# Layer 0 of a two-layer decoder step: the small products between the dense ones moved to three places of every eight, and two kinds of transposes given full shape

## The chip, the core and the metric

The kernel runs on one core of a Trainium2 chip. The metric is the time of one execution on the device in microseconds (us). The core has five engines that work side by side: TensorE (PE, the matrix products), VectorE (DVE), ScalarE (ACT), GpSimd (POOL) and SyncE (SP, which issues most DMA transfers). Each works through its own list of instructions in order; semaphores make one engine wait for another.

## What is computed

One inference step of a decoder with two layers, over 1024 prompt tokens behind 16 meta tokens, and 8 sample sequences of 8 tokens, so 1104 tokens with a model width of 1024. Layer 0, which the change touches, is a gated DeltaNet: one input projection gives q, k (8 heads of 128), v and z (16 heads of 128); q, k and v go through a causal convolution over 4 tokens; then a delta rule runs in chunks, and its outcome is normed, gated with z and projected.

```python
def gdn_mixer(xn, S0, conv_buf, w_in, conv_w, a_log, dt_bias, gn_w, w_out, segments):
    proj = xn @ w_in
    ...
    qkv, new_buf = causal_conv(qkv, conv_buf, conv_w)   # conv_buf: the 3 rows before, of each sequence
    q = l2norm(q) * 128 ** -0.5 ; k = l2norm(k)         # heads repeated: 2 value heads share one key head
    beta = sigmoid(b) ; g = -exp(a_log) * softplus(a + dt_bias)
    o, S = gdn_chunked(q, k, v, g, beta, S, chunk)
    o = rmsnorm(o, gn_w) * silu(z)
    return o @ w_out, S, new_buf

# gdn_chunked, per chunk:
L = strict(kb @ k.T * decay) ; A = L + I                # A is inverted by blocks
v_new = u - w @ S
o = q_dec @ S + attn @ v_new
S = S * exp(g_last) + k_dec.T @ v_new                   # the recurrence from chunk to chunk
```

Layer 1 is an RWKV-7 layer, which the change leaves as it is.

## The kernel before

Layer 0 works through eight pairs of value heads (j = 0 to 7), each pair with its one key head. Tokens lie in three segments of 384, 384 and 336. A pair has six column tiles of the input projection: q of this pair, two tiles of v, two of z, and k of the next pair. A tile of 128 columns and one segment is a **dense product**: eight chunks of the width, three matmuls each (the fp32 numbers are split into a high and a low part, and the product low by low is left out), 24 matmuls with 384 or 336 moving columns. They fill PE nearly without end, and everything else that PE has to do is put between them.

This is done with numbered **gaps**. `dense_gaps` calls `L.gap()` behind each six dense matmuls, and the class `Gaps` then runs what was put at that number, in the order of the priorities given. A pair has 6 x 3 x 4 = 72 gaps; pair j begins at gap B = 24 + 72j. Everything of the small work is a list of such numbers, written by hand:

- the **recurrence** of pair j (`recur_plan`) starts at R0 = B + 60 and takes 8 gaps for each of its nine steps of 128 tokens (6 gaps for j = 7). In a step PE has three places: `rA<-S,K`; three gaps on `rA<-X,TT` and `rA<-S,Q`; two gaps on `rA<-w,ktok`, `rA<-w,attn` and `mktok` (the transpose of K). B is a multiple of eight, so the three are the gap numbers with a remainder of 4, 7 and 1 by eight. DVE makes X (L1039) from the first, the state S (L1072) and o (L1093) from the others, and the next step's `rA<-S,K` reads S.
- `conv_plan` transposes the three history rows of the 8 sample sequences, 24 rows of 128 (`fhist`), and the last rows of each tile, 27 wide (`flast`), and DVE and ACT run the convolution (`cvy`, L634) and SiLU (L641).
- `prep_plan` makes the products of K with itself (`usc`, "squares"), from which DVE takes norms (L752) and E (L766), which go through an inverse by blocks; 18 blocks of 31 and 32 rows are worked on POOL (j > 0) or DVE (j = 0 and the most of 7), and the **merges** (`uU`, `fU`, `uY`, `fY`) put them together with products of 32x32 and 64x64.
- `values_done` transposes v (`f<-vt`); `query_norms` transposes q (`fss`); `sample_read_plan` reads the states of the sample sequences against their keys and queries (`usr`, 128x32 stationary, in four gaps with eight calls each, two passes per call); `sample_write_plan` writes them (`msw`, `fsw`); `msc` are the scores q by k; `gdn_norm_out` transposes o for the norm (`mog`), and DVE gates it (`zg`, L1142).

A product that PE issues goes to one of five kinds of PSUM buffers: "d" (two, dense), "f" (two), "u" (one), "m" (one), "r" (two). The letter at the front of a name in the profile is the kind: `usc` and `usr` both need the single "u". fp32 products issue two passes per call, transposes one.

At the program's start the first rows are normed, and POOL sets T1n (a zeroed buffer for the merges, L708) and kqm (L711) to zero in `gdn_zero`.

Of the kernel before, what the change touches and what calls it, by code (L numbers as in the profile page):

```python
# [25 lines left out]
class Gaps:  # L26
# [62 lines left out]
class Builder:  # L89
# [496 lines left out]
    def conv_plan(self, ends, ft, dst, done=None):  # L586
# [12 lines left out]
        def load():  # L599
            c.hist = t(fp, [24, 128], "hist", 2)  # L600
            nc.sync.dma_start(c.hist, i["state_gdn_conv"][0].rearrange("b r c -> (b r) c")[:, f])

        def head():
            x = t(fp, [128, 411], "raw", 3)
            raws.append(x)
            hp = self.ps("f", 2, "hist")
            self.transpose(hp[:, 0:24], c.hist)
            nc.vector.tensor_copy(v11(x)[:, :, 0:3], v3(hp[:, 0:24]))
            nc.gpsimd.memset(x[:, 88:91], 0.0)
# [13 lines left out]
        def first(s):  # L623
            ys.append(t(fp, [128, 408], "cvy", 2))
            self.act(ys[s][:, 0:wd(s)], raws[s][:, 0:wd(s)], AF.Identity, scale=cw[0])
            if s == 0:
                c.last = t(fp, [128, 27], "last", 2)
                nc.gpsimd.tensor_copy(v3(c.last[:, 0:24]), v11(raws[0])[:, :, 8:11])
            elif s == 2:
                nc.gpsimd.tensor_copy(c.last[:, 24:27], prev(2))  # L630
# [19 lines left out]
        def ending():  # L650
            lp = self.ps("f", 2, "last")
            self.transpose(lp[0:27, 0:128], c.last)
            c.ls = t(fp, [27, 128], "lasts", 1)
            nc.vector.tensor_copy(c.ls, lp[0:27, 0:128])
# [4 lines left out]

        L.put(ends[0] - 11, load, 2)  # L660
        L.put(ends[0] - 2, head, 2)
        for s, e in enumerate(ends):
            L.put(e + 1, lambda s=s: first(s), 1.5)
            L.put(e + 2, lambda s=s: tap(s, 1, 2), 2)
            L.put(e + 3, lambda s=s: tap(s, 3), 2)
            L.put(e + 4, lambda s=s: tanh(s), 2)
            L.put(e + 5, lambda s=s: silu(s), 1.7)
            if done is not None:
                L.put(e + 8, lambda s=s: done(s), 2.2)
        L.put(ends[2] + 5, ending, 2.5)  # L670
        L.put(ends[2] + 8, store, 3)
        return out
# [33 lines left out]
    def gdn_zero(self):  # L706
        self.T1n = self.t(self.fp, [128, 18, 64], "T1n")
        self.nc.gpsimd.memset(self.T1n, 0.0)  # L708
# [23 lines left out]
    def prep_plan(self, j, B, G, o, pace):  # L732
# [11 lines left out]
        def squares(s):  # L744
            if s == 0:
                c.kq, c.rec, c.bp = t(fp, [128, 9], "kq", 2), t(fp, [128, 9], "rec", 2), t(fp, [128, 9, 2], "bp", 2)
            p = p_[s] = self.ps("u", 1, "sc")
            for tt in range(3):
                b = slice(128 * tt, 128 * tt + 128)
                self.mm(p[:, b], G.K[s][:, b], G.K[s][:, b])  # L750
            for tt in range(3):
                nc.vector.scalar_tensor_tensor(p[:, 384:512], p[:, 128 * tt:128 * tt + 128], 1.0, self.ident, op0=ALU.mult, op1=ALU.mult,  # L752
                                               accum_out=c.kq[:, 3 * s + tt:3 * s + tt + 1])
# [22 lines left out]
        for s in range(3):  # L776
# [58 lines left out]
        v = lambda p, k: p[:, 0:6 * k].rearrange("p (c i) -> p c i", i=k)  # L835
        half = lambda s: (("u", 1), ("f", 2), ("u", 1))[s]

        def merge(s):
# [31 lines left out]
            self.act(TT[0:64, :, 64:128], v(p, 64)[0:64], AF.Identity, scale=-1.0)  # L870
        for s, at in enumerate((0, 1, 4)):
            m = merge(s)
            for u in range(4):
                L.put(i0 + 8 + at + u, lambda m=m: next(m, None), 1)
                L.put(i0 + 8 + at + u, lambda m=m: next(m, None), 1.05)

    def values_done(self, G, h, s):
        nc = self.nc
        p = self.ps("f", 2)
        for tt in range(3):  # L880
            self.transpose(p[:, 128 * tt:128 * tt + 128], G.V[:, 128 * tt:128 * tt + 128])
        if h == 0:
# [25 lines left out]
    def sample_read_plan(self, j, B, G):  # L908
# [22 lines left out]
        def out():  # L931
            S = G.sS = t(self.gp, [64, 2, 256], "sS", 1)
            for x in (0, 1):
                nc.scalar.copy(S[:, x], c.ps[64 * x:64 * x + 64, 0:256])
        for g, x in ((12, (0, 0)), (14, (0, 1)), (15, (1, 0)), (22, (1, 1))):
            L.put(B + g, lambda x=x: load(*x), 3)
        L.put(B + 14, spread, 2.6)
        for g, x in ((18, (0, (0, 1))), (19, (0, (2, 3))), (26, (1, (0, 1))), (27, (1, (2, 3)))):
            L.put(B + g, lambda x=x: mults(*x), 2.5)
        L.put(B + 28, out, 2.5)  # L940

    def sample_write_plan(self, j, G, h, r):
# [27 lines left out]
        def store(g):  # L970
            nc.sync.dma_start(self.o["s_gdn"][0, 4 * g:4 * g + 4, hv].rearrange("b k v -> k b v"), Sb[g])
        at = (1, 4 if h else 2, 1, 4, 5, 7, 8, 10, 12) if j < 7 else (1, 2, 1, 3, 4, 5, 5, 7, 9)
        for u, f in zip(at, (lambda: load(0), lambda: load(1), lambda: spread(0, 1, 2, 3), lambda: scale(0, 0, 1), lambda: scale(0, 2, 3),
# [3 lines left out]
    def recur_plan(self, j, R0, G, sp):  # L977
# [1152 lines left out]
    def layer0(self, top, right, xa, xc):  # L2130
# [75 lines left out]
        with tc.manual_schedule(engines=self.every):  # L2206
# [14 lines left out]
            for j, g in enumerate(G):  # L2221
# [462 lines left out]
```

## Time and profile before

| | |
|---|---|
| runs | 2162.58, 2164.77, 2170.14 us, median 2164.77 |
| profiled execution | 2173.22 us, its span 2171.5 us, mean granted clock of PE 0.984 |
| PE busy | 2072.0 us, 95% of the span |
| DVE, ACT, POOL busy | 1483.7 (68%), 1247.0 (57%), 1199.7 us (55%) |
| layer 0's dense products | from about 20 to 1153 us of the span |
| chain that ended last | PE 62%, DVE 17%, DMA 7%, ACT 7% |

The profiled execution is 0.39% over the median. In rows of a timeline, the first number is the start in us, the second the time from the start of the first to the end of the last of the group; a bracket at the end gives how long the engine sat idle before it and what released it. Matmuls overlap, so that the price of a group is read from the starts of its neighbours. L126 is a transpose on PE, L129 a product. `128*32` is the stationary operand, `128x384` the moving one.

### The profile page before, as it was taken

What the parts mean: (1) busy time and instruction counts of PE and PEld (TensorE: products, weight loads), DVE (VectorE), ACT (ScalarE), POOL (GpSimd) and SP (SyncE); (2) the same over time, 40 slices, a digit from 0 to 9 for tenths busy, and PEclk for the clock granted to TensorE, in tenths of its full rate; (3) what the DMA queues carried; (4) which work ended last, traced back from release to release, by engine and by line L of the source; (5) the groups of instructions that cost most, each with busy time, mean ns of one, the idle gap of its engine ahead of it and who ended that gap; (6) DMA issues with size and microseconds to landing.
All of it is one profiled execution on the core that took longest, in us unless ns stands there. A gap on an engine that the chain in (4) does not pass through costs nothing.

```text
span 2171.5 us, 56154 instructions
## 1 busy us (share of the span) xinstructions
PE 2072.0 (95%) x20958; PEld 1935.4 (89%) x20958; DVE 1483.7 (68%) x3761; ACT 1247.0 (57%) x3622; POOL 1199.7 (55%) x1784
## 2 busy tenths in 40 slices
PE   8889999999999999988999999999998989999997
PEld 7879989899898989887999999999888988899886
DVE  7878586675758576795534682578865637899976
ACT  6536565665656565655533374665654437777763
POOL 3418768585858678523432362217866335777751
PEclk9999999999999999999999999999999999999998
DMA  4324242424334242425435225478786576767642
GB/s 123 82 65 129 69 117 79 112 77 119 99 87 121 75 120 75 111 74 163 149 100 150 76 64 175 160 236 249 203 241 180 154 190 180 208 179 194 170 132 88
DMA packets 510764, 291.68 MB, mean 134 GB/s; under 512 B 240777, under 2 KB 495866, under 8 KB 510490
## 3 DMA queue, kind: packets, MB, share of 16 engines
q1 hardware_dynamic: 510490, 288.08, 47.1%
q8 instruction: 166, 2.72, 0.5%
q14 instruction: 108, 0.88, 0.1%
HBM read 195.66 MB, written 92.30 MB: 133 GB/s over the span
## 4 chain that ended last, share of the span: by engine, by line
PE 62%; DVE 17%; DMA 7%; ACT 7%; issue 3%; POOL 2%; SPq 2%; DVEq 0%; POOLq 0%; ACTq 0%
PE d L129 13%; PE dv L129 8%; PE dz L129 7%; PE rA L129 6%; PE do L129 3%; DVE cvy L634 2%; PE rA L133 2%; PE dk L129 2%; PE dq L129 2%; PE zo L129 2%; DMA wraw<-in_gdn_w_out 1%; PE xX L133 1%; DVE invtmp L690 1%; DVE invT L692 1%; PE dlora L129 1%
## 5 line engine op out<-in xcount | busy, mean ns | idle before, releaser
L143 POOL TENSOR_TENSOR wlo<-wraw,whi 128x512 fp32r<-128x512 f32 x174 | 231.9, 1333 | 211.8 <-ACT whi L139 181.0
L634 DVE SCALAR_TENSOR_TENSOR cvy<-raw,cw,cvy 128x408 f32<-128x408 f32 (+2 forms) x288 | 201.0, 698 | 31.5 <-ACT cvy L115 27.6
L692 POOL TENSOR_TENSOR invT<-invT,invtmp 72x31 f32<-72x31 f32 (+27 forms) x310 | 196.3, 633 | 24.3
L690 POOL TENSOR_TENSOR invtmp<-invA,invT 72x31 f32<-72x31 f32 (+27 forms) x310 | 186.9, 603 | 21.7 <-DMA invA<-rltd 3.7
L129 PE MATMUL d<-xc,whi 128*128 128x384 f32 (+1 forms) x640 | 175.8, 340 | 0.5 <-ACT ev L1441 0.5
L139 ACT CAST whi<-wraw 128x512 fp32r<-128x512 f32 x238 | 146.2, 616 | 37.3 <-DMA wraw<-in_rwkv_w_rkvz 14.5
L129 PE MATMUL dv<-xc,whi 128*128 128x384 f32 (+1 forms) x480 | 154.5, 343 | 0.0
L129 PE MATMUL dz<-xc,whi 128*128 128x384 f32 (+1 forms) x480 | 152.0, 339 | 0.0
L115 ACT ACTIVATE w<-rA,nbp 128x128 f32<-128x128 f32 x144 | 45.2, 364 | 152.5 <-PE rA L129 140.0
L129 PEld LDWEIGHTS d<-xc,whi 128*128 128x128 f32 x640 | 117.2, 190 | 2.6 <-ACT ev L1441 0.9
L129 PE MATMUL d<-xc,wlo 128*128 128x384 f32 (+1 forms) x320 | 104.5, 337 | 1.3 <-DVE wlo L143 1.3
L160 POOL TENSOR_TENSOR ors<-ovar,cvals 128x6 f32<-128x6 f32 x24 | 34.1, 1421 | 125.1 <-DVE ovar L1122 125.1
L129 PE MATMUL dv<-xa,whi 128*128 128x384 f32 (+1 forms) x288 | 102.7, 357 | 0.0
L129 PE MATMUL dz<-xa,whi 128*128 128x384 f32 (+1 forms) x288 | 102.1, 354 | 0.5 <-DVE zg L906 0.5
L129 PE MATMUL d<-xa,whi 128*128 128x384 f32 (+1 forms) x336 | 95.4, 337 | 1.1 <-POOL xa L143 1.0
L1953 POOL TENSOR_SCALAR y<-y,mv,grs 128x64 f32<-128x64 f32 x132 | 83.8, 653 | 17.6 <-DVE grs L164 16.0
L959 POOL TENSOR_SCALAR Sb<-Sb,eglb 128x128 f32<-128x128 f32 x128 | 89.5, 711 | 6.4 <-DMA Sb<-in_state_gdn 4.1
L129 PEld LDWEIGHTS dv<-xc,whi 128*128 128x128 f32 x480 | 89.3, 189 | 3.5 <-issue 3.0
L129 PEld LDWEIGHTS dz<-xc,whi 128*128 128x128 f32 x480 | 89.5, 189 | 0.6 <-issue 0.2
L143 DVE TENSOR_TENSOR wlo<-wraw,whi 128x512 fp32r<-128x512 f32 x64 | 49.4, 772 | 50.3 <-ACT whi L139 38.7
L129 PE MATMUL d<-xh,whi 128*128 128x384 f32 (+1 forms) x256 | 82.3, 333 | 0.8 <-ACT xh L139 0.8
L129 PE MATMUL d<-xl,whi 128*128 128x384 f32 (+1 forms) x256 | 82.6, 335 | 0.3 <-DVE sal L1584 0.3
(558 smaller groups left out, 7345.6 us busy)
## 6 DMA issues: line engine op xcount, KB each, us to landing
wraw<-in_gdn_w_in SPq DMA_DIRECT2D x96, 256.0 KB
wraw<-in_rwkv_w_rkvz SPq DMA_DIRECT2D x74, 256.0 KB
Sb<-in_state_gdn SPq DMA_DIRECT2D x64, 256.0 KB
wraw<-in_rwkv_w_o SPq DMA_DIRECT2D x48, 256.0 KB
E<-drow SPq DMA_DIRECT2D x24, 384.0 KB
attn<-drow SPq DMA_DIRECT2D x24, 384.0 KB
wraw<-in_gdn_w_out SPq DMA_DIRECT2D x36, 256.0 KB
out_s_gdn<-Sb SPq DMA_DIRECT2D x32, 256.0 KB
```

The costliest lines, as they stand in the source:

```text
L115: return self.nc.scalar.activation(out, in_, func, bias=bias, scale=scale, **kw)
L129: self.nc.tensor.matmul(out, lhsT, rhs, start=start, stop=stop)
L133: self.nc.tensor.matmul(out, lhsT, rhs, start=start, stop=True, skip_group_check=True)
L139: nc.scalar.copy(hi, x)
L143: e.tensor_tensor(lo, x, hi.bitcast(F32), op=ALU.subtract)
L160: self.nc.gpsimd.tensor_tensor(y, x, half.broadcast_to(sh), op=ALU.pow)
L634: nc.vector.scalar_tensor_tensor(ys[s][:, 0:wd(s)], raws[s][:, k:k + wd(s)], cw[k], ys[s][:, 0:wd(s)], op0=ALU.mult, op1=ALU.add)
L690: v.tensor_tensor(tmp, A[:, j, j + 1:32].unsqueeze(2).broadcast_to([nb, n, m]), Tv[:, j, 0:m].unsqueeze(1).broadcast_to([nb, n, m]), op=AL ...
L692: v.tensor_tensor(Tv[:, j + 1:32, 0:m], Tv[:, j + 1:32, 0:m], tmp, op=ALU.subtract)
L959: nc.gpsimd.tensor_scalar(Sb[g][:, u], Sb[g][:, u], self.eglb[:, hv, 4 * g + u:4 * g + u + 1], None, op0=ALU.mult)
L1953: nc.gpsimd.tensor_scalar(y[:, q], y[:, q], mv[:, q, 0:1], P.rs[:, q:q + 1], op0=ALU.subtract, op1=ALU.mult)
```

## The change

- A helper `on(g)` moves a gap number up to the next with a remainder of 1, 4 or 7 by eight. The transposes of v, the last rows and the query norms are put there.
- The history rows and the last rows get four persistent tiles of 128x128, zeroed by POOL in `gdn_zero`, used in turn. The history product becomes a full product with the tile as stationary operand and 24 columns of the identity moving (two passes instead of one of 24 rows), and `flast` a transpose to 128 rows.
- The squares of segments 0, 1, 2 go from B - 2, B + 2, B + 6 to B - 1, B + 4, B + 7 (j > 0), those of segment 2 into the kind "f".
- The merges of pairs 1 to 6 go from B + 56 to B + 63 (four gaps in a row for each segment, overlapping) to gaps from B + 57 to B + 71, those of segment 2 into "f"; pair 0's go there as well.
- The sample reads take two gaps with 16 calls instead of four with 8; their loads come one gap later.
- The sample writes, the scores and the norm's transposes are shifted by a gap or two, with other priorities, and v has a buffer for each segment.

```diff
+def on(g):
+    while g % 8 not in (1, 4, 7):
+        g += 1
+    return g
...
-            c.hist = t(fp, [24, 128], "hist", 2)
-            nc.sync.dma_start(c.hist, ...)
+            c.hist = self.hists[0]
+            self.hists.reverse()
+            nc.sync.dma_start(c.hist[0:24], ...)
...
-            self.transpose(hp[:, 0:24], c.hist)
+            self.mm(hp[:, 0:24], c.hist, self.ident[:, 0:24])
...
-            self.transpose(lp[0:27, 0:128], c.last)
+            self.transpose(lp[:, 0:128], c.last)
...
-        L.put(ends[0] - 11, load, 2)
-        L.put(ends[0] - 2, head, 2)
+        L.put(max(ends[0] - 11, 3), load, 2)
+        L.put(ends[0] - (3 if ends[0] % 24 == 15 and ft < 16 else 2), head, 2)
...
-                L.put(e + 8, lambda s=s: done(s), 2.2)
-        L.put(ends[2] + 5, ending, 2.5)
-        L.put(ends[2] + 8, store, 3)
+                L.put(on(e + 8), lambda s=s: done(s), 2.2)
+        L.put(on(ends[2] + 5), ending, 2.5)
+        L.put(on(ends[2] + 5) + 3, store, 3)
...
         self.nc.gpsimd.memset(self.T1n, 0.0)
+        self.hists = [self.t(self.fp, [128, 128], f"hist{x}") for x in (0, 1)]
+        self.lasts = [self.t(self.fp, [128, 128], f"last{x}") for x in (0, 1)]
+        for x in self.hists + self.lasts:
+            self.nc.gpsimd.memset(x, 0.0)
...
-            p = p_[s] = self.ps("u", 1, "sc")
+            p = p_[s] = self.ps(*(("f", 2) if j and s == 2 else ("u", 1)), "sc")
...
-            k = B - 2 + 4 * s + o
+            k = B + (-1, 4, 7)[s] if j else B - 2 + 4 * s + o
...
-        for s, at in enumerate((0, 1, 4)):
+        for s in range(3):
             m = merge(s)
-            for u in range(4):
-                L.put(i0 + 8 + at + u, lambda m=m: next(m, None), 1)
+            for u in ((57, 59, 60, 62), (60, 63, 65, 68), (63, 65, 68, 71))[s] if j < 7 else range(...):
+                L.put(B + u, lambda m=m: next(m, None), 2.1 if s and j < 7 else 1)
...
-        for g, x in ((18, (0, (0, 1))), (19, (0, (2, 3))), (26, (1, (0, 1))), (27, (1, (2, 3)))):
+        for g, x in ((20, (0, (0, 1, 2, 3))), (28, (1, (0, 1, 2, 3)))):
             L.put(B + g, lambda x=x: mults(*x), 2.5)
...
-            L.put(T0 - 6, lambda s=s: scores(s), 2)
+            L.put(T0 - (5 if j < 7 else 6), lambda s=s: scores(s), 1.05)
...
-            for h, u in ((0, 9), (1, 11)) if sp == 8 else ((0, 8), (1, 10)):
-                L.put(n0 + u, lambda s=s, h=h: self.gdn_norm_out(j, G, s, h), 2.3)
+            for h, u in ((0, 8), (1, 11)) if sp == 8 else ((0, 8), (1, 10)):
+                L.put(n0 + u, lambda s=s, h=h: self.gdn_norm_out(j, G, s, h), 1.95)
...
-                    L.put(B + 11 + 4 * s, lambda s=s, g=g: self.query_norms(g, s), 2.4)
+                    L.put(on(B + 11 + 4 * s), lambda s=s, g=g: self.query_norms(g, s), 2.4)
```

What this moves is seen at three places. The first is PE's list in pair 4, around the third segment's squares and the scores `msc`. Before, they have a place of their own, ahead of six dense matmuls (`dq`) and the recurrence's `rA<-X,TT`:

```order
2648 L129 MATMUL dq_7505<-xa_100,whi_7260 128x384
2649 L129 MATMUL msc_7561<-Q_5973,K_5647 128x128 x3
2650 L129 MATMUL usc_7566<-K_7522 128x128 x3
2651 L129 MATMUL dq_7505<-xc_104,whi_7260 128x384
2652 L129 MATMUL dq_7505<-xc_104,wlo_7261 128x384
2653 L129 MATMUL dq_7505<-xc_104,whi_7260 128x384 x2
2654 L129 MATMUL dq_7505<-xc_104,wlo_7261 128x384
2655 L129 MATMUL dq_7505<-xc_104,whi_7260 128x384
2656 L129 MATMUL rA_7512<-X_7514,TT_10_118 128x128
2657 L129 MATMUL rA_7513<-X_7515,TT_10_118 128x128
2658 L129 MATMUL rA_7512<-S_7094,Q_5873 128x128
2659 L129 MATMUL rA_7513<-S_7094,Q_5873 128x128
```

Now the same place of PE's list reads:

```order
2653 L136 MATMUL dq_7453<-xc_104,whi_7209 128x384
2654 L136 MATMUL rA_7460<-X_7462,TT_10_118 128x128
2655 L136 MATMUL rA_7461<-X_7463,TT_10_118 128x128
2656 L136 MATMUL rA_7460<-S_6994,Q_5841 128x128
2657 L136 MATMUL rA_7461<-S_6994,Q_5841 128x128
2658 L136 MATMUL msc_7553<-Q_5938,K_5621 128x128 x3
2659 L136 MATMUL fsc_7561<-K_7469 128x128 x3
2660 L136 MATMUL dq_7571<-xa_100,whi_7051 128x336
```

Scores and squares stand one gap later, behind the recurrence's products, and the squares have a buffer of the kind "f". The second place is PE's list at the sample reads of the same pair, of which the first two of a run of eight or sixteen are shown. Before, the second run of eight, behind the transposes of q:

```order
2752 L129 MATMUL usr_7869<-Sb_7727,kqm_420 32x128
2753 L129 MATMUL usr_7869<-Sb_7766,kqm_420 32x128
2754 L129 MATMUL dv_7800<-xc_104,whi_7576 128x384
2755 L129 MATMUL dv_7800<-xc_104,wlo_7577 128x384
2756 L129 MATMUL dv_7800<-xc_104,whi_7576 128x384 x2
2757 L129 MATMUL dv_7800<-xc_104,wlo_7577 128x384
2758 L129 MATMUL dv_7800<-xc_104,whi_7576 128x384
2759 L126 MATMUL fss_7899<-ident_63,Q_7811 128x128 x3
2760 L129 MATMUL usr_7869<-Sb_7727,kqm_420 32x128
2761 L129 MATMUL usr_7869<-Sb_7766,kqm_420 32x128
```

Now all sixteen follow the recurrence's `rA<-S,K`, the norm's transposes and those of q:

```order
2756 L136 MATMUL dv_7859<-xc_104,whi_7428 128x336
2757 L136 MATMUL rA_7866<-S_6994,K_5621 128x128
2758 L136 MATMUL rA_7867<-S_6994,K_5621 128x128
2759 L133 MATMUL mog_7877<-ident_63,o_7135 128x128
2760 L133 MATMUL mog_7877<-ident_63,o_7386 128x128
2761 L133 MATMUL mog_7877<-ident_63,o_7606 128x128
2762 L133 MATMUL fss_7885<-ident_63,Q_7779 128x128 x3
2763 L136 MATMUL usr_7893<-Sb_7698,kqm_426 32x128
2764 L136 MATMUL usr_7893<-Sb_7767,kqm_426 32x128
```

So one visit of the reads stands where two stood, and what was spread over several gaps is in one. The third place is POOL's list at the program's start; rs is a step of the first norms, wlo the low part of a weight. Before:

```order
22 L143 TENSOR_TENSOR wlo_318<-wraw_161,whi_317 128x512
23 L143 TENSOR_TENSOR wlo_322<-wraw_163,whi_321 128x512
24 L160 TENSOR_TENSOR rs_414<-ss_387,cvals_68 128x2
25 L708 MEMSET T1n_418 128x1152
26 L711 MEMSET kqm_420 128x512
27 L321 MEMSET ss_469 128x1
```

Now:

```order
24 L167 TENSOR_TENSOR rs_412<-ss_385,cvals_68 128x2
25 L717 MEMSET T1n_416 128x1152
26 L722 MEMSET hist_86_418 128x128
27 L722 MEMSET hist_87_419 128x128
28 L722 MEMSET last_88_420 128x128
29 L722 MEMSET last_89_421 128x128
30 L725 MEMSET kqm_426 128x512
```

The first history tile is written by a DMA, which now comes after POOL's second memset there.

More of the change, by code (lines that the diff above doesn't have):

```diff
@@ L599, in load @@
         def load():
-            c.hist = t(fp, [24, 128], "hist", 2)
-            nc.sync.dma_start(c.hist, i["state_gdn_conv"][0].rearrange("b r c -> (b r) c")[:, f])
+            c.hist = self.hists[0]
+            self.hists.reverse()
+            nc.sync.dma_start(c.hist[0:24], i["state_gdn_conv"][0].rearrange("b r c -> (b r) c")[:, f])
         def head():
@@ L626, in first @@
             if s == 0:
-                c.last = t(fp, [128, 27], "last", 2)
+                c.last = self.lasts[0]
+                self.lasts.reverse()
                 nc.gpsimd.tensor_copy(v3(c.last[:, 0:24]), v11(raws[0])[:, :, 8:11])
@@ L835, in prep_plan @@
         v = lambda p, k: p[:, 0:6 * k].rearrange("p (c i) -> p c i", i=k)
-        half = lambda s: (("u", 1), ("f", 2), ("u", 1))[s]
+        half = lambda s: (("u", 1), ("f", 2), ("f", 2) if j < 7 else ("u", 1))[s]
         def merge(s):
@@ L870, in merge @@
             self.act(TT[0:64, :, 64:128], v(p, 64)[0:64], AF.Identity, scale=-1.0)
-        for s, at in enumerate((0, 1, 4)):
+        for s in range(3):
             m = merge(s)
-            for u in range(4):
-                L.put(i0 + 8 + at + u, lambda m=m: next(m, None), 1)
-                L.put(i0 + 8 + at + u, lambda m=m: next(m, None), 1.05)
+            for u in ((57, 59, 60, 62), (60, 63, 65, 68), (63, 65, 68, 71))[s] if j < 7 else range(47 + (0, 1, 4)[s], 51 + (0, 1, 4)[s]):
+                L.put(B + u, lambda m=m: next(m, None), 2.1 if s and j < 7 else 1)
+                L.put(B + u, lambda m=m: next(m, None), 2.15 if s and j < 7 else 1.05)
     def values_done(self, G, h, s):
@@ L880, in values_done @@
         for tt in range(3):
-            self.transpose(p[:, 128 * tt:128 * tt + 128], G.V[:, 128 * tt:128 * tt + 128])
+            self.transpose(p[:, 128 * tt:128 * tt + 128], G.V[s][:, 128 * tt:128 * tt + 128])
         if h == 0:
@@ L934, in out @@
                 nc.scalar.copy(S[:, x], c.ps[64 * x:64 * x + 64, 0:256])
-        for g, x in ((12, (0, 0)), (14, (0, 1)), (15, (1, 0)), (22, (1, 1))):
+        for g, x in ((12, (0, 0)), (15, (0, 1)), (16, (1, 0)), (22, (1, 1))):
             L.put(B + g, lambda x=x: load(*x), 3)
         L.put(B + 14, spread, 2.6)
-        for g, x in ((18, (0, (0, 1))), (19, (0, (2, 3))), (26, (1, (0, 1))), (27, (1, (2, 3)))):
+        for g, x in ((20, (0, (0, 1, 2, 3))), (28, (1, (0, 1, 2, 3)))):
             L.put(B + g, lambda x=x: mults(*x), 2.5)
-        L.put(B + 28, out, 2.5)
+        L.put(B + 29, out, 2.5)
     def sample_write_plan(self, j, G, h, r):
@@ L971, in store @@
             nc.sync.dma_start(self.o["s_gdn"][0, 4 * g:4 * g + 4, hv].rearrange("b k v -> k b v"), Sb[g])
-        at = (1, 4 if h else 2, 1, 4, 5, 7, 8, 10, 12) if j < 7 else (1, 2, 1, 3, 4, 5, 5, 7, 9)
+        at = (1, 5 if h else 2, 4 if h else 1, 4, 5, 7, 8, 11, 13) if j < 7 else (1, 2, 1, 3, 4, 5, 5, 7, 9)
         for u, f in zip(at, (lambda: load(0), lambda: load(1), lambda: spread(0, 1, 2, 3), lambda: scale(0, 0, 1), lambda: scale(0, 2, 3),
@@ L2169, in layer0 @@
         for g in G:
-            g.K, g.Q, g.bv, g.zg = {}, {}, {}, ({}, {})
+            g.K, g.Q, g.V, g.bv, g.zg = {}, {}, {}, {}, ({}, {})
         def kept(d, s, tag, n):
@@ L2174, in kept, with values @@
             return d[s]
-        def values(g):
-            g.V = t(self.fp, [128, 384], "vt", 2)
-            return g.V
+        def values(g, s):
+            g.V[s] = t(self.fp, [128, 384], "vt", 2)
+            return g.V[s]
         def begin():
@@ L2254, in layer0 @@
             qc = [self.conv_plan(even(base(j)), j, lambda s, g=g: kept(g.Q, s, "Q", 5)) for j, g in enumerate(G)]
-            vc = [[self.conv_plan(even(base(j) + 12 + 12 * h), 16 + 2 * j + h, lambda s, g=g: values(g),
+            vc = [[self.conv_plan(even(base(j) + 12 + 12 * h), 16 + 2 * j + h, lambda s, g=g: values(g, s),
                                   lambda s, g=g, h=h: self.values_done(g, h, s)) for h in (0, 1)] for j, g in enumerate(G)]
```

## The prediction

> **What bounds the kernel now.** I read the page first, then the windows, the waits, and PE's timeline in one steady pair. The page says that PE is the bound of the whole:
>
> ```profile
> PE 2072.0 (95%) x20958; PEld 1935.4 (89%) x20958; DVE 1483.7 (68%) x3761; ACT 1247.0 (57%) x3622; POOL 1199.7 (55%) x1784
> ```
>
> The windows split layer 0 into two kinds of stretch. After the times stand the busy times of PE, PEld, DVE, ACT, POOL:
>
> ```profile
> 100.00:140.00 40.00, 33.45 (x244) 29.78 (x243) 37.88 (x96) 11.02 (x24) 9.43 (x15) 1.00 0.25 69
> 300.00:420.00 120.00, 118.41 (x1023) 110.39 (x1021) 80.39 (x221) 71.14 (x231) 84.55 (x140) 1.00 0.36 97
> 900.00:970.00 70.00, 62.77 (x447) 56.41 (x446) 67.75 (x189) 39.65 (x132) 29.03 (x45) 1.00 0.31 86
> ```
>
> In a steady pair (300 to 420) PE is idle 1.6 us of 120 and nobody else is near full: there every tenth of PE work counts. In pair 0 (100 to 140) and pair 7 (900 to 970) DVE is busy 37.9 of 40 and 67.8 of 70; PE work saved there is given back as waiting. The steady waits, over about five pairs, are small and named:
>
> ```profile
> PE usc L129 <- DVE E L766: 3.1, 5, 0.6
> PE mktok L126 <- DVE zg L1142: 1.2, 5, 0.3
> PE msc L129 <- DVE Sb L968: 0.8, 5, 0.2
> ```
>
> That is 0.6 + 0.25 + 0.15, about 1.0 us of idle a pair; with the pipe's refilling behind each I put what the waits cost at 1.6 (the idle of the window) to 2.0.
>
> **What a place costs.** The diff gathers small products, so the first question is whether an interruption of the dense stream costs anything by itself. First the undisturbed step, then a history product alone (one instruction), then `rA<-S,K` alone (four), then three groups in one place (eleven):
>
> ```profile
> 440.90 0.34 PE L129 MATMUL dv<-xa,wlo 128*128 128x384 f32 x1
> 441.08 0.33 PE L129 MATMUL dv<-xc,whi 128*128 128x384 f32 x1
> 441.34 0.24 PE L126 MATMUL fhist<-ident,hist 24*128 24x24 f32 x1
> 441.79 0.34 PE L129 MATMUL dv<-xc,wlo 128*128 128x384 f32 x1
> ...
> 439.57 0.34 PE L129 MATMUL dv<-xc,whi 128*128 128x384 f32 x1
> 439.75 0.61 PE L129 MATMUL rA<-S,K 128*128 128x128 f32 x4
> 440.38 0.34 PE L129 MATMUL dv<-xa,wlo 128*128 128x384 f32 x1
> ...
> 443.53 0.33 PE L129 MATMUL dv<-xc,whi 128*128 128x384 f32 x1
> 443.70 0.61 PE L129 MATMUL rA<-X,TT 128*128 128x128 f32 x4
> 444.14 0.61 PE L129 MATMUL rA<-S,Q 128*128 128x128 f32 x4
> 444.59 0.49 PE L126 MATMUL fss<-ident,Q 128*128 128x128 f32 x3
> 445.09 0.34 PE L129 MATMUL dv<-xa,wlo 128*128 128x384 f32 x1
> ```
>
> Dense starts are 441.08 - 440.90 = 0.18 us apart (0.175 over the neighbours). The last row of each piece is the second dense product behind the interruption, so two steps, 0.35, are taken off. History alone: 441.79 - 441.08 - 0.35 = 0.36 for one small instruction. `rA<-S,K`: 440.38 - 439.57 - 0.35 = 0.46, or 0.115 for each of four. Eleven in one place: 445.09 - 443.53 - 0.35 = 1.21, or 0.110 each. So full 128x128 products cost 0.11 each however they are gathered, and **an interruption by them costs nothing of its own**. Shifting `msc`, `mog`, `fss`, the transposes of v and the squares together therefore saves nothing directly. What costs is a product in another shape.
>
> **Last rows.** They have 27 columns already against 128 rows:
>
> ```profile
> 445.80 0.34 PE L129 MATMUL dv<-xc,whi 128*128 128x384 f32 x1
> 445.97 0.27 PE L126 MATMUL flast<-ident,last 128*27 128x128 f32 x1
> 446.26 0.34 PE L129 MATMUL dv<-xa,wlo 128*128 128x384 f32 x1
> ```
>
> 446.26 - 445.80 - 0.35 = 0.11: the price of a full one. Turning it in full shape gains nothing, loses nothing.
>
> **Sample reads.** One visit of sixteen instructions, and the count over the program:
>
> ```profile
> 448.84 0.34 PE L129 MATMUL dv<-xc,wlo 128*128 128x384 f32 x1
> 449.02 0.34 PE L129 MATMUL dv<-xa,whi 128*128 128x384 f32 x1
> 449.29 0.65 PE L129 MATMUL usr<-Sb,kqm 128*32 128x128 f32 x16
> 450.14 0.34 PE L129 MATMUL dv<-xc,wlo 128*128 128x384 f32 x1
> L129 PE MATMUL usr<-Sb,kqm x512: 272/273/298, 107.6 to 946.0; 128*32 128x128 f32 x171
> ```
>
> A visit costs 450.14 - 449.02 - 0.35 = 0.77. One instruction lasts 0.27, the group of sixteen 0.65, so one more costs (0.65 - 0.27)/15 = 0.025 and sixteen 0.41; about 0.35 is the price of coming in another shape, as with history. 512/16 = 32 visits become 16: **-16 x 0.34 = -5.4 us**, two visits or -0.68 in each pair, of which pairs 0 and 7 lie in DVE's stretches.
>
> **History rows.** The count, and the nearest row for the new form (full stationary, 16 moving columns, six instructions):
>
> ```profile
> L126 PE MATMUL fhist<-ident,hist x32: 236/237/240, 30.3 to 942.1; 24*128 24x24 f32 x32
> 1199.23 0.84 PE L129 MATMUL frss<-ones,rsum 128*128 128x16 f32 x6 [1.18 <-DVE rsum L1264]
> 1199.92 0.42 PE L129 MATMUL d<-xh,xa 128*128 128x384 f32 x1
> ```
>
> (1199.92 - 1199.23)/6 = 0.115 each; two passes 0.22. Bounds: 2 x 0.11 if it is a full product, 0.36 + 0.11 if its 24 columns still count as another shape; I take 0.22, as the row with 16 columns is nearest. Standing alone, a history saves 0.36 - 0.22 = 0.14. By the lists of instructions 25 of 32 do; the other seven stand beside sample reads or merges, whose shape they shared, and lose some 0.07 each: 25 x 0.14 - 7 x 0.07 = **-3.0**. Bounds: -4.5 and +3.5. The Trainium skill ("TensorE: Matmul & The Clock Gate", Why this matters for your kernels) says that one product with 32 rows takes the time of one with 128, and that the gain of few rows lies in running several at once. By that rule two passes cost an instruction more than one, 32 x 0.11 = +3.5; the trace's 0.36 against 0.11 for a transpose of full shape speaks against it.
>
> **Merges.** They are in 32x32 and 64x64, now in places of their own with other segments' steps; counted on the two lists with 0.35 for each visit and 0.15 for a change between sizes, they cost +0.2 a pair, **+1.3**. With -5.4 and -3.0 PE's own work falls by 7.1: about -0.85 in each of the pairs 1 to 6 (-5.1), -2 at the ends.
>
> **Waits that go and come.** The first segment's squares no longer stand behind E of another segment in the single "u": the 0.6 goes, `mktok`'s 0.25 and `msc`'s 0.15 too, since their partners move by a gap. That is worth 1.6 to 2.0 a pair. What comes: DVE issues in order, and its list between a pair's first K and S of the fourth step is full. First and last of its 58 rows:
>
> ```profile
> 411.80 0.75 DVE L641 SCALAR_TENSOR_TENSOR K<-raw,cvy 128x64 f32<-128x64 f32 x2 [1.76 <-ACT raw L115]
> 437.95 0.60 DVE L1072 SCALAR_TENSOR_TENSOR S<-S,eglb,rA 128x128 f32<-128x128 f32 x2
> ```
>
> S ends 438.55, PE's `rA<-S,K` at 439.75 needs it: 1.2 us of slack. In the new list a merge's copy (about 0.4) is put ahead, and the squares of the third segment, with `msc`, come a gap later (1.05 of dense, and 0.9 of `rA<-X,TT`, which now stands ahead): their reductions, E and the convolution between stand right ahead of S. Taking the list through with these durations I get S 29.7 us behind the first K (26.75 now) and PE there after 28.2 (27.95 now): a wait of 1.5. `fhist` behind `fss` for a buffer of "f" and `uY` behind its copies add some 0.5. New waits 2.0, old waits 2.0: **the sum for pairs 1 to 6 is 0**, bounds -2.0 and +4 a pair (an engine delay of one whole place, three gaps, 3.2, and 0.5). This is the largest unknown.
>
> **Start.** The first history tile is now zeroed by POOL behind T1n, and SP's transfer has to wait for it, with two weight loads behind it in SP's queue (they are used 20 us later; hidden).
>
> ```profile
> 20.00:42.00 22.00, 19.28 (x109) 16.40 (x108) 19.12 (x44) 12.27 (x25) 8.35 (x10) 0.84 0.25 69
> 30.03 1.06 POOL L708 MEMSET T1n<- 128x1152 f32 x1
> 24.68 0.39 SPq L601 DMA_DIRECT2D hist<-in_state_gdn_conv  x1
> 30.30 0.24 PE L126 MATMUL fhist<-ident,hist 24*128 24x24 f32 x1
> 33.80 1.06 PE L126 MATMUL r<-ident,x 128*128 128x128 f32 x8 [2.01 <-DVE x L347]
> ```
>
> The memset ends about 31.3, the transfer takes 2 to 2.5 us, so `fhist` goes from 30.3 to about 33.6. PE's next wait, for x until 33.80, covers 2.0 of the 3.2; some six dense products (1.05) that stood before that wait stand behind it: +1.0, bounds +0.5 and +2.7 (the granted clock from 20 to 42 is 0.84, the number behind POOL's, and a longer idle stretch could lengthen the slow part). In pair 0 the transposes of v come a gap later, which lets PE run on while DVE is late; the waits are
>
> ```profile
> PE f L126 <- DVE vt L641: 4.7, 3, 2.2
> PE uU L129 <- issue: 1.7, 1, 1.7
> ```
>
> A gap is 1.05: -1.0, and -0.6 at `uU`, whose merge comes later; the PE work saved there is worth -0.4 more. Together the start is -1.0. In pair 7 DVE binds: its PE saving is given back, and pair 6's merges bring DVE some 1 us there: +0.3, bounds 0 and +1.5.
>
> **Sum.** -5.1 (PE work, pairs 1 to 6) + 0 (waits) - 1.0 (start) + 0.3 (pair 7) = -5.8 on the profiled 2173.2, which gives 2167.4. That execution is 0.39% over the median of 2164.8, so on the median **2159 us**. A difference under 0.3%, 6.5 us, can't be told from none here; the forecast lies near that border.
>
> **Rivals.**
> - *DVE keeps up.* If X and E of the third segment land in time, no new waits come, -2.0 x 6 = -12 more: 2147. For it: DVE is busy 80.4 of 120 in the steady window, a third free, and it sits 1.76 idle ahead of 411.80. Against it: the full 27 us just there. 0.23.
> - *S comes late.* The other side: DVE falls behind S by a whole place. From 1.0 us a pair more than I take the gain is gone; at +2.5 us a pair, +15 - 5.8 = +9: 2174. It decides from a new wait of 3.0 us a pair (1.5 in my working). For it: 58 DVE rows, none of which after the first shows an idle time, and the squares' reductions just ahead of S. Against it: priorities that let PE go first by dense work. 0.19.
> - *The change doesn't do what it says.* Pair 7's places (six gaps a step) don't fall on the three remainders, and some merges stand two gaps off them; visits in another shape fall by 16 of the reads alone, and history costs 0.47. Of the reads' -5.4 some -4.1 fall in pairs 1 to 6; +3.5 for history and the waits as reckoned leave about -0.5: 2164. 0.18. The Trainium skill's rule on 32 rows, quoted above, points this way.
>
> The forecast's own case holds 0.40, from 2153 to 2165. With these, faster by over 0.3% (under 2158.3) is 0.23 and half of the forecast's own case, 0.20, and 0.02 of the third rival: 0.45. Slower (over 2171.3) is the second rival's 0.19 less a little: 0.17. Between: 0.38. The range from 2145 to 2173 leaves out the upper half of the second rival and the far end of the first.
>
> **What would show it.** In the changed profile: 16 visits of 32 `usr` in about 1.2 us each; `fhist` as two instructions of 128x24 that cost 0.22 together; `flast` unchanged at 0.11; first `fhist` near 33.6. PE busy in a steady window of 120 us stays near 118, the pair being shorter by 0.85. The waits for E ahead of `usc` are gone, and a wait `rA` <- S of 1 to 2 us stands in each pair's fourth step. If that row is missing and idle is under 1 us a pair, the first rival holds; if it is over 3, the second. What makes me wrong most easily is a wait in DVE's list that I carried through by hand.

## The result, and the profile after

The changed kernel takes 2198.37 us (median of 5, 2192.92 to 2204.94) against 2166.16 of the kernel before (5 runs): a ratio of 1.0141, interval 1.0108 to 1.0174. It is 32 us slower, where 2159 was forecast. The profiled execution took 2204.94 us.

The page, PE's row, and then the windows of the changed kernel: a steady pair, all six steady pairs (180 to 900), and the same of the kernel before. After POOL's busy time stands the granted clock of PE. In rows of the changed kernel L133 is a transpose on PE and L136 a product:

```profile
PE 2087.2 (95%) x20990; PEld 1964.7 (89%) x20990; DVE 1487.7 (68%) x3761; ACT 1246.2 (57%) x3622; POOL 1197.1 (54%) x1788
300.00:420.00 120.00, 116.50 (x997) 110.45 (x996) 78.49 (x215) 69.30 (x226) 82.41 (x137) 0.97 0.33 90
180.00:900.00 720.00, 698.72 (x5858) 663.63 (x5856) 474.51 (x1278) 415.93 (x1347) 490.31 (x814) 0.97 0.35 94
```

```profile
180.00:900.00 720.00, 714.33 (x6155) 667.53 (x6154) 487.35 (x1329) 432.37 (x1398) 513.93 (x841) 1.00 0.36 98
```

Over the whole execution PE is busy a little longer than before (2087.2 us against 2072.0), but in the same 720 us it got less done: 5858 instructions against 6155. There it is idle for 21.3 us instead of 5.7, and the granted clock is 0.97 instead of 1.00, which is worth about another 21 us. A pair, taken as 432 dense products and read from their starts over five pairs, lasts 124.6 us (258.4 to 881.4) instead of 120.3 (253.2 to 854.9). By the same starts layer 0 ends 35 us later: 25 of them come in pairs 1 to 6, 8 in pair 7 and behind it, 1 at the start; layer 1 gives 3 back.

PE's waits between 180 and 920 us (the us in total, the number of times and the longest), and one place where they stand in the timeline:

```profile
PE rA L136 <- DVE o L1107: 16.0, 6, 2.7
PE mktok L133 <- DVE attn L1011: 5.2, 6, 0.9
194.09 0.33 PE L133 MATMUL mktok<-ident,K 128*128 128x128 f32 x1 [0.86 <-DVE attn L1011]
199.97 1.09 PE L136 MATMUL rA<-S,K 128*128 128x128 f32 x4 [2.67 <-DVE o L1107]
201.63 1.22 PE L136 MATMUL msw<-wexp,ktok 32*128 32x512 f32 x1
```

The waits of before (`usc` for E, `msc` for Sb) are gone. In each pair's fourth step PE waits 2.7 us for VectorE's o, and 0.9 us for `attn` some 6 us earlier. Behind the long one the same products take nearly twice their time: `rA<-S,K` 1.09 us where 0.61 was usual. The windows around it show why:

```profile
196.00:198.00 2.00, 1.29 (x8) 0.98 (x6) 1.90 (x9) 0.44 (x1) 2.00 (x2) 1.00 0.38 107
198.00:200.00 2.00, 0.03 (x1) 0.06 (x1) 1.96 (x7) 0.14 (x1) 2.00 (x5) 1.00 0.23 37
200.00:202.00 2.00, 2.00 (x9) 1.67 (x11) 1.61 (x7) 1.81 (x8) 0.32 (x2) 0.52 0.14 21
202.00:204.00 2.00, 2.00 (x5) 0.50 (x4) 0.26 (x1) 1.34 (x6) 0.00 (x0) 0.50 0.78 218
204.00:206.00 2.00, 2.00 (x8) 2.00 (x8) 2.00 (x6) 0.00 (x0) 0.30 (x1) 0.50 0.54 137
206.00:208.00 2.00, 2.00 (x10) 2.00 (x11) 1.84 (x7) 0.00 (x0) 2.00 (x7) 0.77 0.60 186
```

After the idle the granted clock falls to half for about 7 us, which costs 3.4: more than the wait that set it off. Over the six pairs the missing clock, summed over windows of 10 us, is 20.5 us, and it comes in pieces of 1.7, 3.4 or 5.1. The Trainium skill ("TensorE: Matmul & The Clock Gate", Part 1: The HAM clock gate) states that the clock is gated by activity, judged in free-running windows of about 3.4 us, and is halved after an idle window. The pieces, which are one, two or three times half of 3.4, agree with such windows; that a whole window has to be idle does not, since 2.7 us were enough here.

Why VectorE is late is seen in its own timeline. The first row and the last two are the start and the end of the list that the prediction worked through by hand; the others are what matters between:

```profile
169.87 1.14 DVE L650 SCALAR_TENSOR_TENSOR K<-raw,cvy 128x64 f32<-128x64 f32 x2 [0.67 <-ACT raw L122]
183.93 0.51 DVE L650 SCALAR_TENSOR_TENSOR K<-raw,cvy 128x336 f32<-128x336 f32 x1 [2.01 <-ACT raw L122]
184.41 0.27 DVE L766 SCALAR_TENSOR_TENSOR usc<-usc,ident 128x128 f32<-128x128 f32 x1
188.97 1.13 DVE L780 SCALAR_TENSOR_TENSOR E<-usc,bp,E 128x128 f32<-128x128 f32 x4
196.16 1.65 DVE L780 SCALAR_TENSOR_TENSOR E<-fsc,bp,E 128x128 f32<-128x128 f32 x6
199.03 0.60 DVE L1086 SCALAR_TENSOR_TENSOR S<-S,eglb,rA 128x128 f32<-128x128 f32 x2
199.54 0.48 DVE L1107 TENSOR_TENSOR o<-o,rA 128x128 f32<-128x128 f32 x2
```

VectorE works in order. The second segment's squares came two gaps later (B + 4 instead of B + 2), so their reductions (184.41) and E (188.97) no longer fill the time in which VectorE waits for ScalarE's `raw`: it sits idle 2.0 us ahead of 183.93, and all that work then stands between there and S.

### The profile page after: what moved, and what is told of

The parts are those of the page before. It is cut to its first block, busy times and chain, and to the rows that moved or that the text cites. A ratio compares the mean times of both kernels' runs of the same rounds, so it can differ in the third digit from the quotient of the medians.

```text
span 2203.2 us, 56211 instructions
## 1 busy us (share of the span) xinstructions
PE 2087.2 (95%) x20990; PEld 1964.7 (89%) x20990; DVE 1487.7 (68%) x3761; ACT 1246.2 (57%) x3622; POOL 1197.1 (54%) x1788
## 4 chain that ended last, share of the span: by engine, by line
PE 63%; DVE 17%; DMA 7%; ACT 6%; issue 3%; POOL 2%; SPq 2%; DVEq 0%; POOLq 0%; ACTq 0%
PE d L136 14%; PE dv L136 7%; PE dz L136 7%; PE rA L136 6%; PE dk L136 4%; DVE cvy L643 3%; PE rA L140 2%; PE do L136 2%; PE zo L136 2%; DVE E L780 2%; PE xX L140 1%; DMA wraw<-in_gdn_w_out 1%; PE fG L136 1%; DVE invtmp L699 1%; DVE invT L701 1%
## 5 line engine op out<-in xcount | busy, mean ns | idle before, releaser
L136 PE MATMUL d<-xc,whi 128*128 128x384 f32 (+1 forms) x640 | 175.5, 339 | 0.5 <-ACT ev L1455 0.5
L136 PE MATMUL dv<-xc,whi 128*128 128x384 f32 (+1 forms) x480 | 156.8, 350 | 0.0
L136 PE MATMUL dz<-xc,whi 128*128 128x384 f32 (+1 forms) x480 | 149.9, 337 | 0.0
L136 PEld LDWEIGHTS d<-xc,whi 128*128 128x128 f32 x640 | 116.8, 190 | 2.6 <-ACT ev L1455 0.9
L136 PE MATMUL d<-xc,wlo 128*128 128x384 f32 (+1 forms) x320 | 104.3, 336 | 1.0 <-DVE wlo L150 1.0
L136 PE MATMUL dv<-xa,whi 128*128 128x384 f32 (+1 forms) x288 | 104.1, 361 | 0.0
L136 PE MATMUL dz<-xa,whi 128*128 128x384 f32 (+1 forms) x288 | 100.3, 348 | 0.8 <-DVE zg L920 0.8
L136 PE MATMUL d<-xa,whi 128*128 128x384 f32 (+1 forms) x336 | 95.4, 336 | 0.7 <-POOL xa L150 0.7
L136 PEld LDWEIGHTS dv<-xc,whi 128*128 128x128 f32 x480 | 94.3, 199 | 0.0
L136 PEld LDWEIGHTS dz<-xc,whi 128*128 128x128 f32 x480 | 90.1, 191 | 0.2
L973 POOL TENSOR_SCALAR Sb<-Sb,eglb 128x128 f32<-128x128 f32 x128 | 82.8, 659 | 2.0 <-DVE cvy L643 1.1
L136 PE MATMUL d<-xh,whi 128*128 128x384 f32 (+1 forms) x256 | 82.6, 335 | 0.8 <-ACT xh L146 0.8
L136 PE MATMUL d<-xl,whi 128*128 128x384 f32 (+1 forms) x256 | 82.8, 336 | 0.3 <-DVE sal L1598 0.3
L136 PE MATMUL d<-xh,wlo 128*128 128x384 f32 (+1 forms) x256 | 82.3, 335 | 0.0
```

The costliest lines, as they stand in the source:

```text
L136: self.nc.tensor.matmul(out, lhsT, rhs, start=start, stop=stop)
L973: nc.gpsimd.tensor_scalar(Sb[g][:, u], Sb[g][:, u], self.eglb[:, hv, 4 * g + u:4 * g + u + 1], None, op0=ALU.mult)
```

## The experiments

Theory A is that last paragraph with the clock: late squares make S and o late, PE idles, and the low clock behind the idle costs as much again. Rival B is that gathering the small products into few long interruptions is itself the loss.

**One number put back.**

```diff
-            k = B + (-1, 4, 7)[s] if j else B - 2 + 4 * s + o
+            k = B + (-1, 2, 7)[s] if j else B - 2 + 4 * s + o
```

> The changed kernel, with one number put back: the squares of the second segment at B + 2 instead of B + 4 (pairs 1 to 7). Theory A (VectorE reaches the state S late because these squares' reductions and E now stand behind the place where it sat idle 2.0 us; TensorE idles 2.7 us ahead of the fourth step's product by S, and the granted clock falls to 0.5 for 3.4 to 7 us behind each such idle): the idle of 2.7 us a pair falls under 1, the clock stays at 1.00 between 180 and 900 us, and 20 to 30 us come back, 2168 to 2178. Rival B (the loss comes from gathering the small products into few long interruptions): at most 5 us come back, 2193 or more.

Measured: 2162.51 us (10 runs), ratio to before 0.9976 (0.9960 to 0.9991): 36 us come back, more than theory A expected. PE's waits from 180 to 900 and the window:

```profile
PE rA L136 <- DVE o L1107: 6.0, 6, 1.0
PE rA L136 <- DVE X L1053: 1.6, 2, 0.9
180.00:900.00 720.00, 712.30 (x6204) 677.45 (x6203) 496.71 (x1346) 438.11 (x1414) 511.88 (x844) 1.00 0.36 99
```

The wait for o falls from 2.7 to 1.0 us a pair, the one at `mktok` is gone and the clock stays full; the pair lasts 119.1 us. VectorE's list in the same pair as above:

```profile
179.22 0.28 DVE L766 SCALAR_TENSOR_TENSOR usc<-usc,ident 128x128 f32<-128x128 f32 x1
182.38 1.13 DVE L780 SCALAR_TENSOR_TENSOR E<-usc,bp,E 128x128 f32<-128x128 f32 x4
183.42 0.50 DVE L650 SCALAR_TENSOR_TENSOR K<-raw,cvy 128x336 f32<-128x336 f32 x1
194.53 0.59 DVE L1086 SCALAR_TENSOR_TENSOR S<-S,eglb,rA 128x128 f32<-128x128 f32 x2
```

The reductions and E stand ahead of K again, K follows without an idle time, and S ends 27.4 us behind the pair's first K (167.73) instead of 29.8. The places that the change gathered are all still there, so rival B falls. The whole loss hung on where VectorE finds the work of one segment's squares.

**Filling the idle, first try.** Eleven redundant products ahead of the fourth step's `rA<-S,K`, in pairs 0 to 6, written to the same buffer:

```diff
+            if tg == 3 and j < 7:
+                for _ in range(11):
+                    self.mm(c.part(0, 3), self.ident, self.ident)
```

> The changed kernel with 11 more fp32 products of the identity (22 instructions of about 0.11 us, 2.4 us) ahead of the fourth step's product by S in pairs 0 to 6; their result is overwritten. They fill the idle without making S earlier. Theory A with the clock as its larger part: S comes as late as before, the idle falls from 2.7 to about 0.3, the granted clock stays near 1.00 in the steady pairs, and about 3.4 us a pair come back, some 20 in all: 2174 to 2182. Rival C (the idle itself is the loss, and the low clock has another reason): the same time within 5 us, 2193 to 2203, or more by the work added.

Measured: 2199.37 us (2195.95 to 2199.75). The products stood behind the wait, not inside it:

```profile
195.71 2.69 PE L136 MATMUL rA<-ident 128*128 128x128 f32 x22 [2.65 <-DVE o L1110]
198.24 0.61 PE L136 MATMUL rA<-S,K 128*128 128x128 f32 x4
```

The row also tells that the wait is not for S but for the buffer: the two of kind "r" come free when o of the step before has been made, which VectorE does behind S. So this run doesn't test what it was made for, and yet it tells something: the idle is as long, but with 22 full products behind it the clock loss in the six steady pairs falls from 20.5 to 5.1 us, as much as the products add (2.5 a pair).

**Filling the idle, second try.** The same products into a buffer of the kind "m", which is free:

```diff
+            if tg == 3 and j < 7:
+                self.busy("m", 1, 11)
```

> The changed kernel with the 11 extra products of the run before, now into a buffer of the kind m, which is free by then, so that they run inside the idle ahead of the fourth step's product by S (the earlier ones wrote to a buffer of the kind r and waited for the same o). Theory A: S and o as late as before, the idle falls from 2.7 to 0.2 to 0.4, the clock stays at 1.00 in the steady pairs, and what the low clock cost comes back, 20 us in the six steady pairs and some 3 in pair 7: 2173 to 2180. Rival C (the idle is the loss, the clock has another cause): 2193 to 2203.

Measured: 2175.29 us (10 runs), 23 less than the changed kernel, with 17 us of products more in it. The window from 180 to 900, the only wait left there, and the place:

```profile
180.00:900.00 720.00, 714.12 (x6257) 682.22 (x6256) 487.50 (x1309) 425.35 (x1377) 501.28 (x834) 1.00 0.36 98
PE mktok L133 <- DVE attn L1011: 5.1, 6, 1.0
194.03 2.62 PE L136 MATMUL mbusy<-ident 128*128 128x128 f32 x22
196.76 0.71 PE L136 MATMUL rA<-S,K 128*128 128x128 f32 x4
```

The work fills the idle, S is no earlier (29.7 us behind the first K here), the clock stays at 1.00, and the pair falls from 124.6 to 121.3 us. Rival C falls: the low clock is set off by the idle, and is the larger part of what the late S costs.

**The merges put back.** Only their gaps and priorities, to those of before:

```diff
-            for u in ((57, 59, 60, 62), (60, 63, 65, 68), (63, 65, 68, 71))[s] if j < 7 else range(...):
-                L.put(B + u, lambda m=m: next(m, None), 2.1 if s and j < 7 else 1)
...
+            for u in range(i0 - B + 8 + (0, 1, 4)[s], i0 - B + 12 + (0, 1, 4)[s]):
+                L.put(B + u, lambda m=m: next(m, None), 1)
...
```

> The changed kernel with the merges of all pairs at the gaps and priorities of before. Theory A: the wait for S stays, within 0.5 us, since only one copy of 0.4 us leaves VectorE's list ahead of it; 2190 to 2203. Rival B (long interruptions): merges are the longest pieces of them, 10 us or more come back, 2188 or less.

Measured: 2202.38 us (2201.12 to 2206.19), the wait for o 16.3 us in 7 places. The merges have no part in the loss.

**The second segment's squares alone, on the kernel before.**

```diff
-            k = B - 2 + 4 * s + o
+            k = B + (-2, 4, 6)[s] if j else B - 2 + 4 * s + o
```

> The kernel before with one number changed: the squares of the second segment at B + 4 instead of B + 2 (pairs 1 to 7). Theory A: the squares' work moves behind VectorE's idle place and S comes late here too; a wait of 1.5 to 3 us in each pair's fourth step. With an idle over 2.5 us the clock falls and the time is 2180 to 2200; with a shorter one only the wait is added, about 2170 to 2180. Rival B: nothing is gathered, so the time stays within 5 us of 2166.

Measured: 2213.49 us (2206.07 to 2225.83), but not by the wait that theory A names:

```profile
190.57 1.65 PE L129 MATMUL usc<-K 128*128 128x128 f32 x6 [4.83 <-DVE E L766]
```

With all squares in the single "u", the third segment's now wait for E of the second, 4.8 us a pair. The number costs dearly here too, through another buffer; what the run says of S is nothing.

**Between the two numbers.** The squares at B + 3:

> The changed kernel with the second segment's squares at B + 3, between its own B + 4 and the B + 2 that took the loss away. Theory A: the wait for o lies between 1.0 and 2.7 a pair, about 1.8, and the low clock comes less often or not at all; 2166 to 2185. Rival D (it is not the lateness of S but the buffer u, that holds two squares in a row): a jump to one of the ends, within 3 us of 2162 or of 2198.

Measured: 2186.85 us (2182.87 to 2196.38), a little over the expected band. The wait for o is 2.2 us a pair, the clock loss 17 us, the pair 123.0. The time lies between the ends, so rival D (a jump to one of the ends) falls, but the low clock is set off nearly as often by 2.2 us (in five of the six steady pairs) as by 2.7 (in all six); the 2.5 us that the expectation before took as a border was too high.

**E behind S.** The squares left where the change has them, the third segment's E moved behind S and o:

```diff
-            L.put(k + 1, lambda s=s: scaled(s, 0, 1), 2)
-            L.put(k + 2, lambda s=s: scaled(s, 2), 2)
+            late = j and s == 2
+            L.put(B + 10 if late else k + 1, lambda s=s: scaled(s, 0, 1), 2)
+            L.put(B + 10 if late else k + 2, lambda s=s: scaled(s, 2), 2)
```

> The changed kernel with the squares where it has them, but the third segment's E (six VectorE instructions, 1.65 us) put behind S and o of that step instead of ahead of them. Theory A: S and o come 1.65 us earlier, the idle falls from 2.7 to 1.0, and the low clock behind it goes: 2165 to 2176. Rival D (the squares' place and their buffer): no change, 2193 to 2203.

Measured: 2187.54 us (2179.06 to 2197.74). The wait behaves as expected, the clock does not:

```profile
PE rA L136 <- DVE o L1108: 6.0, 6, 1.0
PE mktok L133 <- DVE attn L1012: 5.0, 6, 0.8
195.00:198.00 3.00, 1.99 (x11) 1.39 (x11) 3.00 (x12) 0.81 (x4) 2.76 (x7) 1.00 0.01 3
198.00:201.00 3.00, 3.00 (x9) 1.78 (x7) 2.90 (x11) 2.52 (x9) 0.00 (x0) 0.54 0.21 36
```

1.65 us less work ahead of S takes 1.7 us off the wait, which settles where S is late. But in three of the six pairs the clock still falls (8.5 us in all), although the long idle is gone; in the kernel with the squares at B + 2 a wait of 1.0 us in the same place set it off in none. Among PE's waits what differs is the 0.8 us at `mktok` some 4 us earlier. Behind the idle come transposes and `msw`, `fsw` with 32 rows. That such products count as little activity would fit this and the first fill, but no run here tested it.

**Both.** Squares at B + 2 and E behind S:

> The changed kernel with the second segment's squares at B + 2 and the third segment's E behind S and o. Theory A: the last 1.0 us of wait in each steady pair goes too, six times, so 2154 to 2159, 0.3 to 0.5% under the kernel before. Rival E (PE waits for the next thing in its place): 2160 to 2165.

Measured: 2159.81 us (12 runs), ratio to before 0.9967 (0.9948 to 0.9986), just above the band of theory A. The pair lasts 118.8 us; of waits between 240 and 840 there are left (one more for X, of 1.5 us, stands at 851)

```profile
PE fhist L136 <- ACT fss L122: 1.4, 5, 0.3
PE rA L136 <- DVE X L1054: 0.6, 1, 0.6
```

**Pair 7's idle filled as well.** There VectorE runs an inverse, and what PE saved before had gathered into one wait of 3.1 us ahead of pair 6's sixth step, with the clock at 0.50 behind it:

```diff
+            if tg == 5 and j == 6:
+                self.busy("m", 1, 13)
```

> The kernel with the second segment's squares at B + 2 and the third segment's E behind S, and with 13 redundant products (2.9 us) ahead of the sixth step's product by S of pair 6, where PE idles 3.1 us for o while VectorE works on pair 7's inverse. Theory A: S and o come at the same time, the idle falls to 0.3 or less, and the low clock behind it (near 934 to 940 us) goes, 3.4 us: 2154 to 2158 against the 2159.8 without. Rival F: VectorE is the bound there, so what PE gains is waited for later in the pair: 2158 to 2162.

Measured: 2153.34 us (6 runs), ratio 0.9922 (0.9896 to 0.9949), the lowest median of all; the interval just touches that of the kernel without this fill. Windows at that place without and with the fill:

```profile
934.00:937.00 3.00, 2.77 (x27) 2.41 (x31) 2.83 (x9) 2.29 (x8) 0.00 (x0) 0.50 0.12 36
```

```profile
939.00:942.00 3.00, 2.88 (x47) 2.32 (x45) 2.86 (x9) 2.49 (x9) 0.00 (x0) 1.00 0.26 77
```

The low clock is gone there, but rival F holds in part. PE's waits for o behind 920 us, without and with the fill:

```profile
PE rA L136 <- DVE o L1108: 4.0, 2, 3.1
PE rA L136 <- DVE o L1110: 2.6, 2, 2.4
```

The 3.1 us are filled, and a later wait grows from 0.9 to 2.4: VectorE is the bound of this stretch, so that half of what was filled is waited for again. Pair 7 and as many dense products behind it are 2.9 us shorter in the two profiles (132.2 + 130.1 against 132.8 + 132.4), of which only 0.6 in pair 7 itself; the two kernels' times were not taken on the same chip, so the rest of the 6 us between their medians is not assigned.

**The prices, on the kernel before.** The history rows alone in full shape:

> The kernel before with the history rows alone in full shape (two zeroed tiles of 128x128, a full product with 24 moving columns). By the prediction's rows a history alone falls from 0.36 to 0.22 us, 3.0 us less PE work in layer 0, and the start is about 1.0 us later: 2163 to 2167 against 2166, not to be told from it by the time; the starts of its neighbours decide. By the Trainium skill's rule on 32 rows (TensorE: Matmul & The Clock Gate, Why this matters for your kernels) two passes cost an instruction more, 3.5 us: 0.47 for each, 2170 with the start.

Measured: 2177.54 us (12 runs), ratio 1.0034 (1.0017 to 1.0052): slower by 0.3%, and over the expected band. The price of a history without a wait is what the prediction said. Before (first three rows), and in this run:

```profile
65.61 0.34 PE L129 MATMUL dq<-xc,whi 128*128 128x384 f32 x1
65.87 0.24 PE L126 MATMUL fhist<-ident,hist 24*128 24x24 f32 x1
66.33 0.34 PE L129 MATMUL dq<-xc,wlo 128*128 128x384 f32 x1
```

```profile
64.82 0.34 PE L129 MATMUL dq<-xc,whi 128*128 128x384 f32 x1
65.00 0.30 PE L129 MATMUL fhist<-ident,hist 128*128 128x24 f32 x2
65.40 0.34 PE L129 MATMUL dq<-xc,wlo 128*128 128x384 f32 x1
```

66.33 - 65.61 - 0.35 = 0.37 against 65.40 - 64.82 - 0.35 = 0.23. The rule of the Trainium skill ("TensorE: Matmul & The Clock Gate", Why this matters for your kernels), by which few rows save no time and the two passes would be the dearer form, does not hold for this pair of forms. But in the steady pairs the history now waits for ScalarE's `fss`, and the weight load, 0.13 us long before and 0.30 for the two passes, comes only then:

```profile
436.17 0.40 PE L129 MATMUL fhist<-ident,hist 128*128 128x24 f32 x2 [0.52 <-ACT fss L115]
436.17 0.30 PEld L129 LDWEIGHTS fhist<-ident,hist 128*128 128x128 f32 x2 [0.83 <-ACT fss L115]
```

That place costs 0.65 us more than before, `msc` 0.2 and `fss` 0.3, and the pair goes from 120.3 to 121.1 us. Why ScalarE and VectorE come later against PE there is left open.

The sample reads alone in two places:

> The kernel before with the sample reads alone in two places of 16 calls instead of four of 8. By the prediction's rows each of the sixteen visits left out saves 0.34 us, 0.68 a pair: the steady pairs fall from 120.2 to 119.5 us, 2161 to 2164. If the price of a visit were in the instructions alone, nothing: 2164 to 2168.

Measured: 2162.49 us (12 runs), ratio 0.9966 (0.9945 to 0.9986), the pair 119.6 us: 0.7 us a pair, as worked out. Of the parts that were run alone this is the only one that pays by itself.

## Why the prediction was wrong

The time lies 25 us above the range. Step by step:

- **What a place costs** held: full products are additive, history falls by 0.14, a read's visit costs 0.34. With the squares at B + 2 the pair is 1.2 us shorter than before, near the -0.85 that the PE work was worth.
- **The start** held in its place and fell short in size: `fhist` waits 3.0 us for its DMA and runs at 33.41 (33.6 forecast), but `r<-ident,x` starts at 35.90, 2.1 us later, where +1.0 was taken and +2.7 was the bound; the granted clock is 0.50 there from 33 to 36 us. With pair 0 the start came to about +1 (137.7 against 136.5, by the starts above) where -1.0 was forecast.
- **"New waits 2.0, old waits 2.0: the sum for pairs 1 to 6 is 0"** is the term that failed. It should have been about +5 a pair (124.6 - 120.3 + 0.85). The rows of the pair that lies where the prediction's does, whose first K starts at 419.03:

```profile
448.71 0.60 DVE L1086 SCALAR_TENSOR_TENSOR S<-S,eglb,rA 128x128 f32<-128x128 f32 x2
449.65 1.20 PE L136 MATMUL rA<-S,K 128*128 128x128 f32 x4 [2.67 <-DVE o L1107]
```

S ends 30.3 us behind the first K, where 29.7 was forecast and 26.75 was before: near, but in part by luck. The working lays the delay to a merge's copy and to the third segment's squares, in a list without an idle time; by the run with one number put back (27.9 in this pair) 2.4 of the 3.5 us hang on the second segment's squares, which the working doesn't name, and on the idle time that they leave. PE was there after 27.95 (449.65 - 2.67 - 419.03), as before, and not after 28.2. What frees `rA<-S,K` is o, 0.3 us behind S. These three make a wait of 2.7 out of 1.5. And `mktok` waits for `attn`, 0.9, which was not seen, while the 0.5 at `fhist` and `uY` did not come. That is 3.5 us of idle instead of 2.0.
- **The low clock was left out of that term.** The prediction read clocks under 1 at the start only, and priced idle time in the steady pairs as nothing but idle. It cost 3.4 us a pair on the mean, more than all the error in the waits; 3.5 of new waits less 1.6 to 2.0 of old ones, and 3.4 of clock, are the +5. With it the rival "S comes late", which was given 0.19 and 2174 at most some 2.5 us a pair above the forecast, would have ended near 2189 (2159, 9 for the 1.5 us more of idle in six pairs, 21 for the clock): it was the right rival, priced without what follows the wait. Its sign, over 3 us a pair, was met only with `mktok` counted: the wait named was 2.7.
- **Pair 7** was put at +0.3 and cost 5.2 (136.6 against 131.4). The two waits of the steady pairs come there a seventh time (0.9 us, and 2.65 up to 947.53), with the granted clock at 0.57 from 947 to 955 us, which is 3.4. That is more than the 5.2; VectorE's stretch behind gives some of it back. What PE saved was indeed waited for there in one piece, 3.1 us up to 980.07, but the clock did not fall behind it in this profile (1.00 from 976 to 996 us), as it did in the run with the squares at B + 2 and E behind S.

## What to carry to other kernels

When products of one engine are moved to suit that engine, follow the work that they release on the next one: here two gaps on PE took work out of VectorE's idle time and put it ahead of the value that PE needed next. In this kernel an idle of 2 to 3 us on PE mostly cost about twice its length, since the clock fell behind it (2.7 and 3.4). Several short waits can be cheaper than one long one (the 1.0 us a pair of the kernel before cost no clock, though 0.8 and 1.0 a few us apart did in half of the pairs), and redundant products inside an unavoidable wait can pay for themselves, if they don't wait for the same buffer.

## What was not expected of the hardware

The granted clock fell to 0.5 behind most idle times of 2.1 to 3.1 us between stretches of full work, for 3.4 to 10 us, at a cost of 1.7 to 5.1 us each time. It was not every one: in the changed kernel all six of 2.7 us in the steady pairs had it behind them, but not those of 3.1 (up to 980.07) and 2.4 us in pair 7, and of six of 2.2 us with the squares at B + 3 one had not. 22 full products right behind the idle cut the loss to a quarter (20.5 to 5.1 us over six pairs), and the same 22 inside the idle took it away.
